# The hybrid decoder step with streamed tiles kept in two halves, even and odd tokens, and matmuls that read one of each in turn

## The chip, the cores and the metric

The kernel runs on one core of one Trainium2 chip. The metric is the device time of one execution in microseconds. Engines are named as the profile names them: PE is TensorE (PEld its weight loads), DVE VectorE, ACT ScalarE, POOL GpSimd, SP the queue that issues most DMAs.

## What is computed

One step of a decoder layer for 256 prompt tokens and 8 x 4 sample tokens, all float32, 2048 wide, feed-forward width 5632:

```
x = x + 1/2 * SwiGLU_1(rmsnorm(x))
h = rmsnorm(x);  z = h @ w_in            # columns: ssm u | q | k | v
y_ssm  = S5 scan of u, gelu, GLU
y_attn = sliding-window attention (window 128), 16 q heads, 4 kv heads
x = x + w_out @ concat(rmsnorm(y_ssm), rmsnorm(y_attn))
x = x + 1/2 * SwiGLU_2(rmsnorm(x))
```

The outputs are the new x, the key and value caches and the states of the scan.

## The kernel before

The activations lie transposed: 128 features on the partitions, the N = 288 tokens along each partition. x is 16 such tiles (KT = 16). All weights come from memory in 680 pieces of 128 x 1024 elements or less, in the order of use; class `Weights` loads each piece (SP queue), and splits it into a rounded high part wh (ScalarE, L89) and a rest wl (VectorE, L90), both of the type fp32r.

Each activation that is multiplied with weights is split likewise. `split_x` does it for x with the norm's gain (xh by ScalarE, L181; xl by VectorE, L182), `up` inside `ffn` for the hidden units (h by VectorE, L308; hh by ScalarE, L309; hl by VectorE, L310), `y_split` inside `mix` for the two mixers' outputs (L678 and L684). A product of a weight and an activation is then three matmuls into one PSUM tile, `mm3` (L273 to L275): wh with the high part, wh with the rest, wl with the high part. The weight block of 128 x 128 is the stationary operand, the activation tile, 288 columns, is the moving one. Every weight block is used for one tile of columns, so each matmul has a weight load beside it.

The stages, in order, are the first SwiGLU (`ffn(0)`, in four chunks of hidden units, each with its part of the down projection), the combined projection with the scan and the attention between its matmuls (`mix`), the output projection, and the second SwiGLU (`ffn(1)`). The order on every engine is that in which the program is written; side work (norms, tables of the scan, softmax) is hung into slots between weight pieces by `Weights.at` and `Weights.spread`. All of `mm3`'s calls stand in `projs`, `down` and the loop over w_out at the end of `mix`. The matmuls of the scan and the attention don't go through `mm3`; they read tiles of their own.

Of the rest of the names: e, p and c5 belong to the tables of the scan (`precompute`), where `er`, `ei` and `c5` hold five powers side by side for each of 32 states, so that `er[:, :, 1]` is 32 elements five apart; `QS` (tile qs) holds the sample tokens' queries with a sequence's elements sixteen apart.

Of the kernel before, what the change touches and what calls it, by code (L numbers as in the profile page):

```python
# [10 lines left out]
F32 = mybir.dt.float32  # L11
F32R = mybir.dt.float32r
I32 = mybir.dt.int32
AF = mybir.ActivationFunctionType
ALU = mybir.AluOpType
# [10 lines left out]
N = T * W1  # L26
# [11 lines left out]
SLOPES = [float(np.float32(2.0 ** (-8.0 * (h + 1) / NH))) for h in range(NH)]  # L38
MAGIC = 1.5 * 2.0 ** 23
TWO_PI = 6.283185005187988  # L40


def heads_of(i):
# [74 lines left out]
def tile_hymba_step(ctx, tc, io):  # L118
    nc = tc.nc
    act, dve, pool_e, pe, sp = nc.scalar, nc.vector, nc.gpsimd, nc.tensor, nc.sync  # L120
# [12 lines left out]
    def ffn_units(l):  # L133
        seq = []
        for c in range(NCK):
            for f in range(CHS[c]):
                if not (c > 0 and f == 0):
                    seq.append(("gu", C0[c] + f))
            if c + 1 < NCK:
                seq.append(("gu", C0[c + 1]))  # L140
            seq.append(("down", c))
        return seq
# [26 lines left out]
    x = [cp.tile([P, N], F32, name="x%d" % k) for k in range(KT)]  # L169
    xh = [cp.tile([P, N], F32R, name="xh%d" % k) for k in range(KT)]  # L170
    cp.tile([P, 32], F32, name="gap_x")
    xl = [cp.tile([P, N], F32R, name="xl%d" % k) for k in range(KT)]
    gains = cp.tile([P, 66], F32, name="gains")
# [4 lines left out]
    cp.tile([P, 56], F32, name="gap_w")  # L178

    def split_x(k, g):  # L180
        act.activation(xh[k], x[k], AF.Copy, scale=gains[:, g:g + 1])  # L181
        dve.scalar_tensor_tensor(xl[k], x[k], gains[:, g:g + 1], xh[k].bitcast(F32),  # L182
                                 op0=ALU.mult, op1=ALU.subtract)

    def square_x(k, first=False, eng=pool_e, acc=acc):
# [72 lines left out]
    for k in range(8):  # L258
        split_x(k, k)
    W.split()  # L260
    W.split()
    for k in range(8, KT):
        split_x(k, k)
# [5 lines left out]
    def mm3(ps, wh, wl, kts, rh, rl, first, last):  # L269
        n = len(kts)  # L270
        for a, k in enumerate(kts):
            s = slice(a * P, (a + 1) * P)
            pe.matmul(ps, wh[:, s], rh[k], start=first and a == 0, stop=False)  # L273
            pe.matmul(ps, wh[:, s], rl[k], start=False, stop=False)  # L274
            pe.matmul(ps, wl[:, s], rh[k], start=False, stop=last and a == n - 1)  # L275

    def projs(n):

        ps = [pm.tile([P, 512], F32, name="main") for _ in range(n)]
        for hf in range(2):  # L280
            for p_ in ps:
                wh, wl = W.next()
                mm3(p_[:, :N], wh, wl, range(8 * hf, 8 * hf + 8), xh, xl, hf == 0, hf == 1)
        return ps

    def proj():
        return projs(1)[0]

    def ffn(l, post, hp, first):
        HH, HL = {}, {}  # L290
        w0 = W.i
        hold = Hold(W.i + first)
        early = [] if l else projs(3)

        def gate(f, pg, s2):
            t1 = tp.tile([P, N], F32, name="t1")
            s1 = tp.tile([P, N], F32, name="s1")
            dve.tensor_tensor(t1, pg[:, :N], R, op=ALU.mult)  # L298
            act.activation(s1, t1, AF.Silu)  # L299
            pool_e.tensor_tensor(s2, s1, R, op=ALU.mult)  # L300

        def up(f, pu, s2):
            h = tp.tile([P, N], F32, name="h")
            hh = hp.tile([P, N], F32R, name="hh")
            if f == 0:
                hp.tile([P, 32], F32, name="gap_r", bufs=1)
            hl = hp.tile([P, N], F32R, name="hl")
            dve.tensor_tensor(h, pu[:, :N], s2, op=ALU.mult)  # L308
            act.copy(hh, h)  # L309
            dve.tensor_tensor(hl, h, hh.bitcast(F32), op=ALU.subtract)  # L310
            HH[f], HL[f] = hh, hl

        def gu(f):
            s2 = tp.tile([P, N], F32, name="s2")
            pg = early.pop(0) if early else proj()
            hold(lambda: gate(f, pg, s2))
            pu = early.pop(0) if early else proj()
            hold(lambda: up(f, pu, s2))

        def down(c):  # L320
            n = CHS[c]
            rh = {k: HH.pop(C0[c] + k) for k in range(n)}
            rl = {k: HL.pop(C0[c] + k) for k in range(n)}
            for d in range(KT):
                ps = pm.tile([P, 512], F32, name="main")
                wh, wl = W.next()
                mm3(ps[:, :N], wh, wl, range(n // 2), rh, rl, True, False)
                wh, wl = W.next()
                mm3(ps[:, :N], wh, wl, range(n // 2, n), rh, rl, False, True)
                dve.scalar_tensor_tensor(x[d], ps[:, :N], 0.5, x[d], op0=ALU.mult, op1=ALU.add)  # L330
                if c == NCK - 1:
                    post(d)

        def gap():

            ps = pm.tile([P, 512], F32, name="main")
            for i in range(2):
                pe.matmul(ps[:, :256], ones, R[:, 8:264], start=i == 0, stop=i == 1)

        W.at(w0 + first + 8, gap)  # L340
        for kind, j in ffn_units(l):
            (gu if kind == "gu" else down)(j)
# [8 lines left out]
    def precompute(qp):  # L351
# [65 lines left out]
        def cos_sin(c, s, f, tmp):  # L417
            act.activation(s, f, AF.Sin, scale=TWO_PI)
            stt(tmp, f, -1.0, f, op0=ALU.mult, op1=ALU.max)
            yield  # L420
            act.activation(c, tmp, AF.Sin, bias=halfpi, scale=-TWO_PI)

# [15 lines left out]
        def common():  # L438
# [34 lines left out]
            yield from cos_sin(c5, ei, f5, g5)  # L473
            act.activation(shalf, f5[:, :, 1], AF.Sin, scale=TWO_PI / 2)
            yield
# [124 lines left out]
    def post_norm(g0):  # L600
        def prep(d):
            split_x(d, g0 + d)
            square_x(d, d == 0)

        def post(d):
            W.at(W.i + (d < KT - 1), prep, d)
        return post
# [10 lines left out]
    with ExitStack() as es:  # L618
        mix(tc, nc, io, es, W, MIX0, dict(
            x=x, xh=xh, xl=xl, gains=gains, ident=ident, ones=ones, acc=acc, R=R, tp=tp,  # L620
# [11 lines left out]
def mix(tc, nc, io, es, W, base, e):  # L632
    act, dve, pool_e, pe = nc.scalar, nc.vector, nc.gpsimd, nc.tensor
    tt, ts, stt = dve.tensor_tensor, dve.tensor_scalar, dve.scalar_tensor_tensor
    x, R, gains, ident, acc = e["x"], e["R"], e["gains"], e["ident"], e["acc"]
# [36 lines left out]
    def y_split(pool, src, g, first, eng=pool_e):  # L672
        hh = pool.tile([P, N], F32R, name="hh", bufs=8)
        if first:
            pool.tile([P, 32], F32, name="gap_y", bufs=1)
        hl = pool.tile([P, N], F32R, name="hl", bufs=8)
        gc = gains[:, g:g + 1]
        act.activation(hh, src, AF.Copy, scale=gc)  # L678
        YH.append(hh)
        YL.append(hl)  # L680
        sq = tp.tile([P, N], F32, name="sq", bufs=3)
        act.activation(sq, src, AF.Square)
        yield
        stt(hl, src, gc, hh.bitcast(F32), op0=ALU.mult, op1=ALU.subtract)  # L684
        if first:
            eng.tensor_copy(acc, sq)
        else:
            eng.tensor_tensor(acc, acc, sq, op=ALU.add)
# [102 lines left out]
    def ssm_glu(j):  # L791
        yn = YN.pop(j)
        ps = aux()
        pe.matmul(ps[:, :N], GL.pop(j), yn, start=True, stop=True)
        t = tp.tile([P, N], F32, name="s1")
        act.activation(t, ps[:, :N], AF.Tanh, scale=0.5)
        yield
        y2 = tp.tile([P, N], F32, name="s2")
        stt(y2, t, 1.0, yn, op0=ALU.add, op1=ALU.mult)
        yield  # L800
        yield from y_split(ys, y2, 48 + j, j == 0, dve if j == 7 else pool_e)
# [14 lines left out]
    for j in range(8):  # L816
        s = base + 2 * j + 5
# [50 lines left out]
    for j in range(8):  # L868
        ps = proj()
# [13 lines left out]
    for p in range(2):  # L883
        ps = proj()
# [120 lines left out]
    def sample(p):  # L1005
# [56 lines left out]
        for g in range(4):  # L1062
            act.copy(tok(YR[4 * p + g], None), src[:, g])
        yield
        todo = [y_split(lp, YR.pop(4 * p + g), 56 + 4 * p + g, p == 0 and g == 0) for g in range(4)]
        for g in range(5):
            for y in todo[max(0, g - 1):g + 1]:
# [3 lines left out]
    for i in range(8):  # L1071
        s = base + 2 * (12 + i) + 2
# [4 lines left out]
    for p in range(2):  # L1077
        s = base + 2 * (12 + 4 * p + 3) + 2
# [4 lines left out]
    for i in range(8):  # L1083
        p, g = divmod(i, 4)
        ps = proj()
# [16 lines left out]
    for hf in range(2):  # L1102
        for d in range(KT):
            if hf and d == 1:
                W.at(W.i, att_norm)
            wh, wl = W.next()
            ps = pm.tile([P, 512], F32, name="main")
# [163 lines left out]
```

## Time and profile before

| | |
|---|---|
| median of 3 runs | 1998.19 us (1997.27 to 2003.86) |
| span of the profiled execution | 1998.1 us |
| instructions | 37634 |
| TensorE busy | 1980.5 us, 99% |
| VectorE, ScalarE, GpSimd busy | 1219.0, 852.0, 296.0 us |
| moved by DMA | 359.04 MB, mean 180 GB/s |

No time besides the span is listed for the profiled execution itself, so the span is what the working below starts from. In a row of a group stand line, engine, operation, output and inputs with their shapes, the count, then busy time in us and the mean of one in ns, then the idle time of the engine before them and what ended it. A row of a stretch has, for each engine, the busy us and the number of instructions, then the granted clock of TensorE, the share of the DMA engines and the GB/s. A row of the timeline has the start and the length in us. Matmuls overlap, so their lengths add up to more than the time they take; the distance of their starts is what one costs.

### The profile page before, as it was taken

The page shows a single profiled execution, that of the slowest core. Times are in us where ns is not written, and L with a number is a line of the kernel's source. Part 1 is how long each engine was busy: PE and PEld are TensorE (multiplying, and loading weights), DVE is VectorE, ACT ScalarE, POOL GpSimd, SP SyncE. Part 2 cuts the span into 40 slices and gives each one's busy share as a digit, 9 for nine tenths or more (in the row PEclk, how much of TensorE's full clock was granted, in tenths as well). Part 3 has the DMA queues.
Part 4 walks back from the last instruction along what each step waited for, and adds up shares of the span by engine and source line. Part 5 has one row for each costly group of instructions (what it writes and reads, how often), then busy time and mean ns, then how long its engine had stood idle before and what let it go on. Part 6 is the DMA issues. An engine that isn't in the chain of part 4 may idle for free.

```text
span 1998.1 us, 37634 instructions
## 1 busy us (share of the span) xinstructions
PE 1980.5 (99%) x15256; PEld 1968.0 (98%) x15256; DVE 1219.0 (61%) x1874; ACT 852.0 (43%) x1334; POOL 296.0 (15%) x450
## 2 busy tenths in 40 slices
PE   8999999999999999999999999999999999999999
PEld 7999999999999999999989999999999999999999
DVE  5577666566666654677888874555555455555554
ACT  5443444443444443543476553333333333333333
POOL 3110011000100000211368640000000000000000
PEclk9999999999999999999999999999999999999999
DMA  7555655546555664678744445555555555555555
GB/s 237 188 169 152 198 168 201 193 151 209 198 180 155 215 201 142 216 248 265 247 132 132 154 159 169 169 155 172 181 169 162 160 186 169 157 157 193 169 154 158
DMA packets 122622, 359.04 MB, mean 180 GB/s; under 512 B 22448, under 2 KB 30256, under 8 KB 121264
## 3 DMA queue, kind: packets, MB, share of 16 engines
q1 hardware_dynamic: 114672, 340.81, 53.5%
q10 hardware_dynamic: 7776, 15.83, 2.3%
q8 instruction: 119, 1.95, 0.4%
q14 instruction: 55, 0.45, 0.1%
HBM read 338.40 MB, written 20.22 MB: 179 GB/s over the span
## 4 chain that ended last, share of the span: by engine, by line
PE 96%; DMA 1%; POOL 1%; DVE 0%; SPq 0%; ACT 0%; issue 0%; POOLq 0%; ACTq 0%; DVEq 0%
PE main L273 31%; PE main L275 31%; PE main L274 31%; POOL acc L191 1%; PE main L733 1%; DMA yd<-yg 0%; PE main L566 0%; PE main L572 0%; DMA x<-in_x 0%; PE main L988 0%; DMA raw<-in_w_gu 0%; PE main L775 0%; PE main L774 0%; PE main L956 0%; PE main L773 0%; PE main L975 0%
## 5 line engine op out<-in xcount | busy, mean ns | idle before, releaser
L90 DVE TENSOR_TENSOR wl<-raw,wh 128x1024 fp32r<-128x1024 f32 (+2 forms) x680 | 758.6, 1116 | 526.2 <-ACT wh L89 521.1
L273 PE MATMUL main<-xh,wh 128*128 128x288 f32 x3136 | 924.4, 295 | 6.7 <-ACT xh L181 6.4
L275 PE MATMUL main<-xh,wl 128*128 128x288 f32 x3136 | 919.0, 293 | 2.2 <-DVE wl L90 2.2
L274 PE MATMUL main<-xl,wh 128*128 128x288 f32 x3136 | 918.4, 293 | 0.6 <-DVE xl L182 0.6
L89 ACT CAST wh<-raw 128x1024 fp32r<-128x1024 f32 (+2 forms) x680 | 643.1, 947 | 600.2 <-PE main L274 385.4
L273 PEld LDWEIGHTS main<-xh,wh 128*128 128x128 f32 x3136 | 589.5, 188 | 8.0 <-ACT xh L181 6.4
L275 PEld LDWEIGHTS main<-xh,wl 128*128 128x128 f32 x3136 | 589.3, 188 | 3.0 <-DVE wl L90 2.9
L274 PEld LDWEIGHTS main<-xl,wh 128*128 128x128 f32 x3136 | 589.5, 188 | 1.4 <-DVE xl L182 1.0
L273 PE MATMUL main<-hh,wh 128*128 128x288 f32 x1664 | 489.8, 294 | 0.0
L274 PE MATMUL main<-hl,wh 128*128 128x288 f32 x1664 | 487.9, 293 | 0.3 <-DVE hl L684 0.3
L275 PE MATMUL main<-hh,wl 128*128 128x288 f32 x1664 | 487.8, 293 | 0.0
L274 PEld LDWEIGHTS main<-hl,wh 128*128 128x128 f32 x1664 | 312.6, 188 | 0.7 <-DVE hl L684 0.5
L273 PEld LDWEIGHTS main<-hh,wh 128*128 128x128 f32 x1664 | 312.5, 188 | 0.5 <-DVE t L1095 0.2
L275 PEld LDWEIGHTS main<-hh,wl 128*128 128x128 f32 x1664 | 312.5, 188 | 0.0
L300 POOL TENSOR_TENSOR s<-s,R 128x288 f32<-128x288 f32 x88 | 71.3, 810 | 1228.0 <-ACT s L299 1228.0
L299 ACT ACTIVATE s<-t 128x288 f32<-128x288 f32 x88 | 39.2, 445 | 233.5 <-DVE t L298 233.5
L309 ACT CAST hh<-h 128x288 fp32r<-128x288 f32 x88 | 38.2, 434 | 235.5 <-DVE h L308 235.5
L330 DVE SCALAR_TENSOR_TENSOR x<-main,x 128x288 f32<-128x288 f32 x128 | 58.4, 456 | 52.3 <-PE main L275 51.1
L308 DVE TENSOR_TENSOR h<-main,s 128x288 f32<-128x288 f32 x88 | 40.2, 457 | 70.3 <-PE main L275 69.9
L298 DVE TENSOR_TENSOR t<-main,R 128x288 f32<-128x288 f32 x88 | 40.2, 457 | 59.4 <-PE main L275 59.2
L310 DVE TENSOR_TENSOR hl<-h,hh 128x288 fp32r<-128x288 f32 x88 | 40.3, 458 | 44.0 <-ACT hh L309 44.0
L191 POOL TENSOR_TENSOR acc<-acc,sq 128x288 f32<-128x288 f32 x45 | 48.4, 1075 | 45.8 <-ACT sq L187 44.4
(266 smaller groups left out, 891.0 us busy)
## 6 DMA issues: line engine op xcount, KB each, us to landing
raw<-in_w_gu SPq DMA_DIRECT2D x352, 512.0 KB, 3.5
raw<-in_w_dn SPq DMA_DIRECT2D x128, 384.0 KB, 3.0
raw<-in_w_dn SPq DMA_DIRECT2D x128, 320.0 KB, 3.0
raw<-in_w_in SPq DMA_DIRECT2D x40, 512.0 KB, 4.7
raw<-in_w_out SPq DMA_DIRECT2D x32, 512.0 KB, 3.4
mats<-stage ACTq DMA_DIRECT2D x8, 1536.0 KB, 7.1
mb<-mats SPq DMA_DIRECT2D x8, 768.0 KB, 5.3
ma<-mats SPq DMA_DIRECT2D x8, 512.0 KB, 4.2
```

The lines of the kernel that those rows point to most:

```text
L89: self.nc.scalar.copy(wh[:, :n], t[:, :n])
L90: self.nc.vector.tensor_tensor(wl[:, :n], t[:, :n], wh[:, :n].bitcast(F32), op=ALU.subtract)
L191: eng.tensor_tensor(acc, acc, sq, op=ALU.add)
L273: pe.matmul(ps, wh[:, s], rh[k], start=first and a == 0, stop=False)
L274: pe.matmul(ps, wh[:, s], rl[k], start=False, stop=False)
L275: pe.matmul(ps, wl[:, s], rh[k], start=False, stop=last and a == n - 1)
L298: dve.tensor_tensor(t1, pg[:, :N], R, op=ALU.mult)
L299: act.activation(s1, t1, AF.Silu)
L300: pool_e.tensor_tensor(s2, s1, R, op=ALU.mult)
L308: dve.tensor_tensor(h, pu[:, :N], s2, op=ALU.mult)
L310: dve.tensor_tensor(hl, h, hh.bitcast(F32), op=ALU.subtract)
L330: dve.scalar_tensor_tensor(x[d], ps[:, :N], 0.5, x[d], op0=ALU.mult, op1=ALU.add)
```

## The change

A tile that the matmuls stream (xh, xl, hh, hl, and the h from which the last two are made) no longer holds its 288 tokens in order. Its first 144 elements are the tokens with even numbers, its last 144 those with odd numbers. The instructions that write these tiles read their sources at every second element (`evens`) and write two runs (`halved`). In `mm3` the moving operand is read through `woven`: element 0 of the first half, element 0 of the second, element 1 of the first, and so on, so that the columns enter the array, and the sums leave it, in the order of tokens as before. x, R, the norms and everything that reads PSUM are as they were. The number of instructions, their order on every engine, the tiles and the DMAs are the same. Line numbers after the change are higher by 15 from L43 on.

```diff
+def evens(ap):
+    return ap.rearrange("p (b a) -> p a b", a=2)
+
+def halved(ap):
+    return ap.rearrange("p (a b) -> p a b", a=2)
+
+def woven(ap):
+    return ap.rearrange("p (a b) -> p b a", a=2)
...
     def split_x(k, g):
-        act.activation(xh[k], x[k], AF.Copy, scale=gains[:, g:g + 1])
-        dve.scalar_tensor_tensor(xl[k], x[k], gains[:, g:g + 1], xh[k].bitcast(F32),
+        act.activation(halved(xh[k]), evens(x[k]), AF.Copy, scale=gains[:, g:g + 1])
+        dve.scalar_tensor_tensor(halved(xl[k]), evens(x[k]), gains[:, g:g + 1], halved(xh[k].bitcast(F32)),
                                  op0=ALU.mult, op1=ALU.subtract)
...
-            pe.matmul(ps, wh[:, s], rh[k], start=first and a == 0, stop=False)
-            pe.matmul(ps, wh[:, s], rl[k], start=False, stop=False)
-            pe.matmul(ps, wl[:, s], rh[k], start=False, stop=last and a == n - 1)
+            pe.matmul(ps, wh[:, s], woven(rh[k]), start=first and a == 0, stop=False)
+            pe.matmul(ps, wh[:, s], woven(rl[k]), start=False, stop=False)
+            pe.matmul(ps, wl[:, s], woven(rh[k]), start=False, stop=last and a == n - 1)
...
-            dve.tensor_tensor(h, pu[:, :N], s2, op=ALU.mult)
+            dve.tensor_tensor(halved(h), evens(pu[:, :N]), evens(s2), op=ALU.mult)
...
-        act.activation(hh, src, AF.Copy, scale=gc)
+        act.activation(halved(hh), evens(src), AF.Copy, scale=gc)
...
-        stt(hl, src, gc, hh.bitcast(F32), op0=ALU.mult, op1=ALU.subtract)
+        stt(halved(hl), evens(src), gc, halved(hh.bitcast(F32)), op0=ALU.mult, op1=ALU.subtract)
```

## The prediction

> **What bounds the kernel now.** I read the page's busy line, clock line and chain first, then the groups by line, then one stretch, then single instructions in it.
>
> ```profile
> span 1998.1 us, 37634 instructions
> ...
> PE 1980.5 (99%) x15256; PEld 1968.0 (98%) x15256; DVE 1219.0 (61%) x1874; ACT 852.0 (43%) x1334; POOL 296.0 (15%) x450
> ...
> PEclk9999999999999999999999999999999999999999
> ...
> PE 96%; DMA 1%; POOL 1%; DVE 0%; SPq 0%; ACT 0%; issue 0%; POOLq 0%; ACTq 0%; DVEq 0%
> ```
>
> TensorE is busy from end to end, its granted clock is full in every slice, and 96% of the chain that ended last is TensorE itself. Its idle time in the whole run is 1998.1 - 1980.5 = 17.6 us. The next engine, VectorE, is at 61%. The sum below is made against this span, 1998.1 us; the median of the three runs, 1998.19 us, is the same to 0.01%.
>
> ```profile
> L273 PE MATMUL main<-xh,wh 128*128 128x288 f32 x3136 | 924.4, 295 | 6.7 <-ACT xh L181 6.4
> L275 PE MATMUL main<-xh,wl 128*128 128x288 f32 x3136 | 919.0, 293 | 2.2 <-DVE wl L90 2.2
> L274 PE MATMUL main<-xl,wh 128*128 128x288 f32 x3136 | 918.4, 293 | 0.6 <-DVE xl L182 0.6
> L273 PE MATMUL main<-hh,wh 128*128 128x288 f32 x1664 | 489.8, 294 | 0.0
> L274 PE MATMUL main<-hl,wh 128*128 128x288 f32 x1664 | 487.9, 293 | 0.3 <-DVE hl L684 0.3
> L275 PE MATMUL main<-hh,wl 128*128 128x288 f32 x1664 | 487.8, 293 | 0.0
> ```
>
> These six groups are all the calls of `mm3`: 3 x 3136 + 3 x 1664 = 14,400 matmuls of 288 columns. Every one of them reads its moving operand in the new order after the change. The mean of 293 ns is the length of one instruction, and they overlap, so what one costs the kernel is read from their starts. A stretch of the second SwiGLU, and three neighbours in it:
>
> ```profile
> 1300.00:1500.00 200.00, 200.00 (x1541) 200.00 (x1540) 101.05 (x119) 75.48 (x92) 8.10 (x10) 1.00 0.55 169
> ...
> 1500.05 0.29 PE L273 MATMUL main<-xh,wh 128*128 128x288 f32 x1
> 1500.18 0.29 PE L274 MATMUL main<-xl,wh 128*128 128x288 f32 x1
> 1500.31 0.29 PE L275 MATMUL main<-xh,wl 128*128 128x288 f32 x1
> ```
>
> 1541 matmuls in 200 us are 129.8 ns from start to start, with no idle time on TensorE and the DMA engines at 55%. So 14,400 x 0.1298 = 1869 us of the span is `mm3`, and 129 us is everything else (the small matmuls of the scan and the attention, and the 17.6 us of idle time). A change in the cost of one streamed column is a change of 14,400 x 288 columns: 0.01 ns on each is 41 us.
>
> How much of the 129.8 ns belongs to the columns? The first matmuls of the run go at another pace:
>
> ```profile
> 8.05 0.44 PE L275 MATMUL main<-xh,wl 128*128 128x288 f32 x1
> ...
> 12.13 0.44 PE L274 MATMUL main<-xl,wh 128*128 128x288 f32 x1
> ```
>
> They are 17 steps apart, 4.08 / 17 = 240 ns each, for the same 288 columns: 0.833 ns a column, just what two array steps would be if the steady pace were 120 ns of columns and 10 ns of something fixed. I take that reading: 0.417 ns a column (120 ns) and about 10 ns besides.
>
> **The change, part by part.** It removes no instruction, adds none and moves none; every engine's list reads as before. What it alters is where elements lie and in which order they are read.
>
> (1) The matmuls' reads. Before, one column follows the other in the tile. Now two columns in succession come from places 144 elements apart, one of each half. No matmul of the run before reads so: all its moving operands are runs of 16 elements and more, but for the two-column ones of L946, which are too short to price. So the price has to be bounded.
>
> From below: if TensorE takes elements from anywhere at the same pace, the cost is 0. Below nothing too: the fixed 10 ns might come from neighbours being read too closely behind each other; taking them all away gives 14,400 x 0.0098 = 141 us less.
>
> From above, the nearest rows are on VectorE. These instructions all handle 32 elements; each pair does the same work, but one member has its 32 elements five apart in the tile (`er[:, :, 1]`, `c5[:, :, 1]`, tile p) or sixteen apart (tile qs), the other has them side by side:
>
> ```profile
> L396 DVE TENSOR_TENSOR p<-tmps,tmpi 128x32 f32<-128x32 f32 x1 | 0.2, 216 | 0.0
> L396 DVE TENSOR_TENSOR s<-tmps,tmpi 128x32 f32<-128x32 f32 x1 | 0.2, 191 | 0.0
> L480 DVE TENSOR_TENSOR tmps<-s,p 128x32 f32<-128x32 f32 x1 | 0.2, 213 | 0.0
> L449 DVE TENSOR_TENSOR s<-prm,s 128x32 f32<-128x32 f32 x1 | 0.2, 189 | 0.0
> L1090 DVE TENSOR_TENSOR qs<-main,R 128x32 f32<-128x32 f32 x8 | 1.6, 202 | 0.0
> L886 DVE TENSOR_TENSOR vT<-main,R 128x32 f32<-128x32 f32 x2 | 0.3, 175 | 0.0
> L310 DVE TENSOR_TENSOR hl<-h,hh 128x288 fp32r<-128x288 f32 x88 | 40.3, 458 | 44.0 <-ACT hh L309 44.0
> ```
>
> Scattered elements cost 25 ns (writing), 24 ns (reading) and 27 ns (writing) more for 32, so about 0.78 ns an element. Side by side an element costs (458 - 191) / (288 - 32) = 1.04 ns. Scattered, the same engine is slower by a factor of 1.75: 1.8 ns an element. This can be carried over to TensorE in three ways:
> - by the ratio: 0.417 x 1.75 = 0.73 ns a column, 210 + 10 = 220 ns a matmul;
> - by the addition: 0.417 + 0.78 = 1.2 ns, 345 + 10 = 355 ns;
> - by the time of one access: 1.8 ns, 518 + 10 = 528 ns.
>
> That last one, 14,400 x (0.528 - 0.1298) = 5734 us more, is the upper end.
>
> I take one element per two array steps: 0.833 ns a column, 240 + 10 = 250 ns. [...] With the fixed part hidden it is 240 ns, with all of the 129.8 ns doubled 260 ns.
>
> [...]
>
> Sum for (1): 14,400 x (250 - 129.8) ns = 1731 us, all on the path, since TensorE waits for nothing in between.
>
> (2) The edits on VectorE and ScalarE that put the halves in place (L181, L182, L308, L678, L684): their inputs are now read at every second element, their outputs written in one run.
>
> ```profile
> L182 DVE SCALAR_TENSOR_TENSOR xl<-x,gains,xh 128x288 fp32r<-128x288 f32 x48 | 32.8, 710 | 0.0
> L308 DVE TENSOR_TENSOR h<-main,s 128x288 f32<-128x288 f32 x88 | 40.2, 457 | 70.3 <-PE main L275 69.9
> L684 DVE SCALAR_TENSOR_TENSOR hl<-s,gains,hh 128x288 fp32r<-128x288 f32 x14 | 10.4, 744 | 0.0
> L181 ACT ACTIVATE xh<-x,gains 128x288 fp32r<-128x288 f32 x48 | 24.1, 529 | 3.9 <-POOL x L1096 3.1 <-DVE x L330 0.6
> ```
>
> At best they cost nothing; at worst 288 x 0.78 = 225 ns each, by the same VectorE rows: 48 + 88 + 16 = 152 instructions, 34 us on VectorE, and 64 instructions (L181, L678), 14 us on ScalarE. In the stretch above VectorE is free for 99 of 200 us and ScalarE for 125, and TensorE's matmuls would leave them twice that. I cost them at nothing. Without that cover, at the start and at the turns between stages, it is a few instructions of 0.2 us, 2 us in all.
>
> (3) The 129 us besides: the small matmuls read as before. Of the 17.6 us of idle time some goes if the stream is slower, since weights then come early: 0 to 17.6 us less. I count 0.
>
> Sum: 1998.1 + 1731 = 3729 us.
>
> **The rivals.**
>
> *No price (not slower).* [...] Then a matmul stays at 129.8 ns, the time at 1998 us within the 0.3% (6 us) that this kernel's measurement can tell from no change; and if the fixed 10 ns goes as well, 1857 us. It decides as soon as the starts stay below 130 ns. [...]
>
> *Part of a price.* Reads run ahead in the 10 ns, or pairs are served together, and a matmul ends between 131 and 235 ns; with the ratio's 220 ns the time is 1998 + 14,400 x 0.0902 = 3297 us. [...]
>
> *A dearer access.* The time of one access counts and not the engine's step. At 355 ns it is 5241 us, at 528 ns 7732 us. For it speaks that 25 ns in 32 elements was seen on three different instructions, whether reading or writing, so it may belong to the memory; against it that the stream now takes a column in 0.417 ns. It also comes to pass if TensorE, idle at every second step, falls back to the pace of its first microseconds (240 instead of 129.8 ns for the same matmul): every step then doubles, 500 ns, 7329 us. [...]
>
> **How the numbers follow.** Half pace, 240 to 260 ns (3585 to 3873 us): 0.46. Part of a price, 2004 to 3585 us: 0.15. A dearer access, above 3873 us: 0.24. No price: 0.12 within 0.3%, and 0.03 faster. The likeliest gives 3729 us, its own range being 3585 to 3873. For the whole I leave out the no-price cases (0.15), the smallest part-prices below 2300 us (0.02) and what lies above 7200 us (0.03): 2300 to 7200 us. Slower is 0.46 + 0.15 + 0.24 = 0.85, the same 0.12, faster 0.03.
>
> **What would show it.** In the trace after, the starts of neighbouring matmuls in the second SwiGLU decide between all cases: 240 to 260 ns for my forecast, 129.8 for the rival without a price, 355 or about 500 for the dearer ones. A stretch of 200 us should hold some 800 matmuls, TensorE should stay busy from end to end, VectorE's and ScalarE's shares should about halve. L308's and L182's counterparts may grow by up to 225 ns without a wait of TensorE on them. If the small matmuls or the waits of TensorE on VectorE took up the difference, step (2) or (3) would be wrong; if the granted clock fell, part of a rival.

## The result and the profile after

The changed kernel takes 1890.03 us (median of 4 runs, 1888.15 to 1892.07). Its ratio to the kernel before is 0.9454, 95% interval 0.9439 to 0.9469: 5.5% faster, where 3729 us were forecast. Before has one run of 2424.86 us among its four; the ratio leaves it out.

The page after, its span, busy line and chain:

```profile
span 1888.7 us, 37634 instructions
...
PE 1864.6 (99%) x15256; PEld 1850.5 (98%) x15256; DVE 1208.9 (64%) x1874; ACT 850.2 (45%) x1334; POOL 301.1 (16%) x450
...
PE 92%; DVE 2%; POOL 2%; DMA 1%; ACT 1%; issue 1%; SPq 0%; POOLq 0%; ACTq 0%; DVEq 0%
```

The same number of instructions, TensorE still busy from end to end, and 109.4 us less. A stretch of the first SwiGLU, the stretch of the second that was shown of before, and three neighbours behind it:

```profile
200.00:400.00 200.00, 200.00 (x1628) 199.69 (x1628) 133.86 (x220) 91.65 (x144) 23.99 (x36) 1.00 0.61 199
1300.00:1500.00 200.00, 200.00 (x1635) 200.00 (x1634) 107.09 (x124) 80.15 (x99) 9.60 (x12) 1.00 0.59 180
...
1500.42 0.29 PE L288 MATMUL main<-hh,wh 128*128 128x288 f32 x1
1500.55 0.29 PE L289 MATMUL main<-hl,wh 128*128 128x288 f32 x1
1500.67 0.29 PE L290 MATMUL main<-hh,wl 128*128 128x288 f32 x1
```

1635 matmuls stand where 1541 stood: 122.3 ns from start to start instead of 129.8. (A stretch also counts a matmul that is under way at its start, so such quotients read up to some 0.6 ns low; averaged start by start, this stretch has 122.5 and 130.0 ns.) 14,400 x 7.5 ns = 108 us is nearly all of the difference. The rest of the run, 1888.7 - 14,400 x 0.1223 = 128 us, is about what it was (129 us). Two smaller things nearly cancel in this sum: the first SwiGLU gained more than 7.5 ns a matmul (1628 in the stretch from 200 to 400 us, where 1523 stood before), and TensorE's idle time grew from 17.6 to 24.1 us (1888.7 - 1864.6). At 0.417 ns a column, which the runs of other widths show below ((162.4 - 122.4) / 96 ns), the columns take 120 ns: 7.5 of the 10 ns that stood beside them are gone, and 2.5 are left.

### The profile page after: what moved, and what is told of

Same layout as the page of the kernel before. It is cut to its first block, busy times and chain, and to the rows that moved or that the text cites. A ratio compares the mean times of both kernels' runs of the same rounds, so it can differ in the third digit from the quotient of the medians.

```text
span 1888.7 us, 37634 instructions
## 1 busy us (share of the span) xinstructions
PE 1864.6 (99%) x15256; PEld 1850.5 (98%) x15256; DVE 1208.9 (64%) x1874; ACT 850.2 (45%) x1334; POOL 301.1 (16%) x450
## 4 chain that ended last, share of the span: by engine, by line
PE 92%; DVE 2%; POOL 2%; DMA 1%; ACT 1%; issue 1%; SPq 0%; POOLq 0%; ACTq 0%; DVEq 0%
PE main L288 30%; PE main L290 30%; PE main L289 29%; DVE wl L105 1%; ACT wh L104 1%; PE main L748 1%; DMA U<-ud 0%; DMA ud<-t 0%; POOL acc L206 0%; PE main L581 0%; PE main L587 0%; POOL x L1111 0%; DMA raw<-in_w_gu 0%; PE main L789 0%; PE main L790 0%
## 5 line engine op out<-in xcount | busy, mean ns | idle before, releaser
L288 PE MATMUL main<-xh,wh 128*128 128x288 f32 x3136 | 904.4, 288 | 7.0 <-ACT xh L196 6.4
L290 PE MATMUL main<-xh,wl 128*128 128x288 f32 x3136 | 898.6, 287 | 3.0 <-DVE wl L105 3.0
L289 PE MATMUL main<-xl,wh 128*128 128x288 f32 x3136 | 898.4, 286 | 0.6 <-DVE xl L197 0.6
L288 PE MATMUL main<-hh,wh 128*128 128x288 f32 x1664 | 478.0, 287 | 1.3 <-DVE t L1110 0.7
L289 PE MATMUL main<-hl,wh 128*128 128x288 f32 x1664 | 476.0, 286 | 0.6 <-DVE hl L699 0.6
L290 PE MATMUL main<-hh,wl 128*128 128x288 f32 x1664 | 476.0, 286 | 0.0
L323 DVE TENSOR_TENSOR h<-main,s 128x288 f32<-128x288 f32 x88 | 40.1, 455 | 55.5 <-PE main L290 55.1
```

What stands on the lines that cost most here:

```text
L288: pe.matmul(ps, wh[:, s], woven(rh[k]), start=first and a == 0, stop=False)
L289: pe.matmul(ps, wh[:, s], woven(rl[k]), start=False, stop=False)
L290: pe.matmul(ps, wl[:, s], woven(rh[k]), start=False, stop=last and a == n - 1)
L323: dve.tensor_tensor(halved(h), evens(pu[:, :N]), evens(s2), op=ALU.mult)
```

## Experiments

**Which half of the change.** Two kernels take it apart, and a third reads in turn without storing halves.

The first leaves tiles in order and only reads them through `woven`:

```diff
-            pe.matmul(ps, wh[:, s], rh[k], start=first and a == 0, stop=False)
+            pe.matmul(ps, wh[:, s], woven(rh[k]), start=first and a == 0, stop=False)
...
```

> Only the order of the matmuls' reads is changed; the tiles keep their tokens in order, so the sums come out for other tokens than they should. If the order of reading is the cause (theory A: a plain read loses time at places it crosses as it runs on, which reading from two far places in turn hides; theory B: a matmul's start is shortened by that order): 122.3 ns from start to start and about 1889 us. If the placing by VectorE and ScalarE is the cause (theory C): 129.8 ns and 1998 us.

The second stores halves as the changed kernel does and reads them in one run (in `mm3`, `woven(rh[k])` becomes `rh[k]` again).

> The tiles are stored in halves, but the matmuls read them as one run, so the sums come out for other tokens than they should. Theories A and B: 129.8 ns and 1998 us. Theory C: 122.3 ns and 1889 us.

Measured: 1889.26 us (ratio 0.9446, 0.9432 to 0.9461) and 1998.36 us (ratio 0.9989, 0.998 to 0.9999). The same stretch in both, reads first, then writes:

```profile
1300.00:1500.00 200.00, 200.00 (x1635) 200.00 (x1635) 106.97 (x125) 80.61 (x99) 9.61 (x12) 1.00 0.57 179
```

```profile
1300.00:1500.00 200.00, 200.00 (x1541) 200.00 (x1540) 100.72 (x118) 75.49 (x92) 8.10 (x10) 1.00 0.54 169
```

The order of reading is the whole effect; storing halves costs and gives nothing that the measurement can tell. Theory C is out.

The third kernel reads pairs in turn and lets the sums fall into PSUM in the same order, so that nothing has to be stored differently:

```diff
-            pe.matmul(ps, wh[:, s], rh[k], start=first and a == 0, stop=False)
+            pe.matmul(turns(ps), wh[:, s], turns(rh[k]), start=first and a == 0, stop=False)
...
+def turns(ap):
+    return ap.rearrange("p (a b c) -> p b a c", a=2, c=2)
```

> Tiles stay in order and VectorE and ScalarE are as before; the matmuls read two elements of each half in turn and write the sums to PSUM in the same order, so that each lands in its own column. If pairs hide what single elements hide and PSUM takes the pairs without delay: 122.3 ns, 1888 us, as fast as the changed kernel. If only single elements in turn help, or if the sums' scattered writing costs as much: 129.8 ns, 1998 us. If scattered writing halves the pace: 240 ns, 3580 us.

Measured: 2769.62 us, ratio 1.3848 (1.3828 to 1.3869). None of the three expectations. Its stretch:

```profile
1900.00:2300.00 400.00, 400.00 (x2165) 400.00 (x2164) 141.93 (x165) 106.81 (x130) 12.07 (x15) 1.00 0.38 121
```

400 us / 2165 = 184.8 ns a matmul. The map of turns below has pairs read in turn with PSUM in order, and 184.7 ns too: it is the reading of pairs that costs, and PSUM takes sums scattered by pairs without a delay that shows beside it. Whether it takes single sums scattered as well, which would have spared the stored halves, no run tried.

**Which orders are cheap.** In the next four kernels only the second SwiGLU is altered, and each ran once; what is read from them are distances within one trace, at a granted clock of 1.00. Every 38 weight pieces `mm3` takes another order, each on a line of its own, for instance

```diff
+                elif seg == 1:  # step 2
+                    pe.matmul(ps[:, :N], w, r.rearrange("p (b a) -> p a b", a=2), start=st, stop=sp_)
```

> Only in the second SwiGLU, each eighth of its weight pieces has another order of reading (its sums are those of other tokens): plain; every 2nd, 4th, 8th, 16th, 48th element and then the next sweep; one of each half in turn; one of each quarter in turn. Distance of starts expected. Plain 129.8 ns, halves 122.3. Theory A with one lost step of 0.417 ns for every 16 elements crossed (18 in 288 make 7.5 ns): step 2: 122.3 + 36 x 0.417 = 137; step 4: 152; step 8: 182; steps 16 and 48: 242; quarters 122.3. Theory B (lost at the start alone): 129.8 or 122.3 for all steps. The price forecast for reads that never use a neighbour: 250 ns from step 4 on.

The rows are answers for one line each: count, shortest, median and longest of one matmul, then first and last start. One operand's matmul is every third, so the distance of starts is (last - first) / 3 / (count - 1). In order: every 2nd, 4th, 8th, 16th, 48th element, halves in turn, quarters in turn. (The first order, plain, is the stretch of 80 us ahead of them.)

```profile
1205.00:1285.00 80.00, 80.00 (x618) 80.00 (x617) 40.80 (x46) 30.73 (x39) 4.86 (x6) 1.00 0.50 169
...
L281 PE MATMUL main<-hh,wh x144: 438/438/438, 1374.1 to 1484.3; 128*128 128x288 f32 x144
L283 PE MATMUL main<-hh,wh x48: 440/442/443, 1485.0 to 1521.9; 128*128 128x288 f32 x48
L285 PE MATMUL main<-xh,wh x144: 421/422/423, 1711.1 to 1816.2; 128*128 128x288 f32 x144
L287 PE MATMUL main<-hh,wh x72: 423/425/427, 1905.2 to 1957.7; 128*128 128x288 f32 x72
L289 PE MATMUL main<-hh,wh x120: 334/335/336, 2168.4 to 2227.9; 128*128 128x288 f32 x120
L291 PE MATMUL main<-hh,wh x40: 286/286/294, 2228.4 to 2242.7; 128*128 128x288 f32 x40
L293 PE MATMUL main<-hh,wh x160: 316/316/318, 2353.4 to 2426.5; 128*128 128x288 f32 x160
```

Plain 129.4 ns; step 2: 257; step 4: 262; step 8: 245; step 16: 246; step 48: 167; halves 122; quarters 153. Scattered reads do cost what the forecast said, 245 to 262 ns against 250. Halves in turn, though not one column lies beside the one before, are no scattered read. Theory A's steps (137, 152, 182, and 122.3 for quarters) and theory B's (one value for all) both fail. The elements crossed don't set the price, since step 2 (257 ns) costs no less than step 16 (246 ns).

> Only in the second SwiGLU, each eighth of its weight pieces is read in another way (wider matmuls repeat the first tokens into columns that nothing uses; with other weights the sums are wrong). Distance of starts. Plain, 288, 384 and 512 columns: if the 7.5 ns are lost along the way, 18 steps for 288 columns, one for each 16 (theory A): 129.8, 172.3, 228.9 ns; if they are lost once at the start (theory B): 129.8, 169.8, 223.1. Halves in turn, 288, 384, 512 columns: 122.3, 162.3, 215.6 by both. [...]

Plain with 384 and 512 columns, halves with 288, 384 and 512, weights at every 8th element (gate and up projections), at every 5th (down projection) and at every 2nd:

```profile
L281 PE MATMUL main<-hh,wh x144: 336/337/338, 1347.6 to 1422.7; 128*128 128x384 f32 x144
L283 PE MATMUL main<-hh,wh x48: 390/391/393, 1423.2 to 1455.7; 128*128 128x512 f32 x48
L285 PE MATMUL main<-hh,wh x120: 286/286/286, 1674.9 to 1718.6; 128*128 128x288 f32 x120
L287 PE MATMUL main<-hh,wh x72: 326/326/326, 1719.0 to 1753.6; 128*128 128x384 f32 x72
L289 PE MATMUL main<-hh,wh x120: 379/379/379, 1928.0 to 2005.1; 128*128 128x512 f32 x120
L291 PE MATMUL main<-xh,wh x240: 401/404/415, 2032.9 to 2206.6; 128*128 128x288 f32 x120
L291 PE MATMUL main<-hh,wh x40: 307/388/398, 2005.7 to 2032.2; 128*128 128x288 f32 x40
L293 PE MATMUL main<-hh,wh x160: 292/295/298, 2226.5 to 2289.9; 128*128 128x288 f32 x160
```

Plain: 175 and 230 ns; halves: 122.4, 162.4 and 216.0, so 0.417 ns for each column from 288 to 384 and 0.419 from there to 512. The difference is 7.5 ns at 288 columns, 12.6 at 384 and 14 at 512: it grows with the columns, and theory B, which had 223 at 512, is out. It doesn't grow in step with them (the wider matmuls read 192 or 256 elements twice), and theory A's 172.3 and 228.9 are missed by 3 and 1 ns. There is one weight load per matmul at each width, and the difference grows all the same; whether the load has a part in it stays open, since a stream without weight loads was not run. Weights with a step come out unevenly beside the 129.8 ns of plain ones: 133 ns where four blocks of five are read at every 2nd, 227 at every 5th and 242 at every 8th.

> Only in the second SwiGLU, each eighth of its weight pieces has another order of moving reads (sums of other tokens): runs of 2, 4, 8 and 16 elements from each half in turn; then single elements in turn from two neighbouring blocks of 4, 8, 16 and 48 elements. The step map gave 257, 262, 245, 246 ns for steps 2, 4, 8, 16, 167 for step 48, 153 for quarters, 122.3 for halves. Reuse theory (a pair of neighbours is fetched for two columns' time; a few fetched pairs are kept while other places are read, so with two places in turn each pair is still fetched once, with 18 places it is lost before its second use): all eight orders 122 to 130 ns. Bank theory (two columns in succession collide when their places share a bank, near ones do, those 144 apart don't): runs 122 to 130; neighbouring blocks of 4, 8, 16 like the steps 4, 8, 16: 262, 245, 246; of 48 like step 48: 167.

Runs of 2, 4, 8, 16 from each half, then neighbouring blocks of 4, 8, 16, 48 in turn:

```profile
1205.00:1335.00 130.00, 130.00 (x704) 129.90 (x703) 45.80 (x52) 36.20 (x45) 5.62 (x7) 1.00 0.35 117
...
L281 PE MATMUL main<-hh,wh x144: 302/302/303, 1384.0 to 1442.7; 128*128 128x288 f32 x144
L283 PE MATMUL main<-hh,wh x48: 299/302/303, 1443.1 to 1462.3; 128*128 128x288 f32 x48
L285 PE MATMUL main<-hh,wh x120: 302/302/302, 1620.2 to 1669.0; 128*128 128x288 f32 x120
L287 PE MATMUL main<-hh,wh x72: 286/286/287, 1669.4 to 1695.5; 128*128 128x288 f32 x72
L289 PE MATMUL main<-hh,wh x120: 286/286/286, 1813.5 to 1857.2; 128*128 128x288 f32 x120
L291 PE MATMUL main<-hh,wh x40: 286/286/286, 1857.6 to 1871.9; 128*128 128x288 f32 x40
L293 PE MATMUL main<-hh,wh x160: 286/286/286, 1978.1 to 2036.5; 128*128 128x288 f32 x160
```

Runs: 184.7, 137, 136 and 137 ns. Blocks: 122.4 for all four. Distance is of no account: turns between elements 4 apart are as good as 144 apart, so the bank theory falls. The reuse theory (122 to 130 ns for all eight) holds for the blocks, but is at least 55 ns off for runs of 2 and 6 for the longer runs.

**What a cheap order has in common.** Write the columns as pairs, 0.83 ns each at 0.417 ns a column. Halves: (0,144) (1,145) (2,146) (3,147), four pairs on the same two groups of four neighbours, then two new groups. Plain: (0,1) (2,3), two pairs on a group, then the next. Step 2 and more: every pair on a new group. Theory L counts just that, theory P only that there are two places in turn. Pairs and groups of four are a way of counting that sorts the measured orders; no run shows them in the engine. Groups of two don't sort: halves (122.4 ns) and blocks of 2 (129.4 ns, below) would both have two pairs on a group. Nor do groups of eight: plain (129.8 ns) and blocks of 4 (122.4 ns) would both have four.

> Only in the second SwiGLU, each eighth of its weight pieces has another order of moving reads (sums of other tokens). Two theories fit most orders so far. Theory P: two places in turn hide a loss that one running place shows. Theory L: columns are taken two at a time; a pair that needs a line of four neighbours other than the pair ahead waits one double step (0.83 ns) unless a pair that stays on its lines stands behind it, and even then a little; so each line should serve four pairs in a row (halves) rather than two (plain), and one pair for each line costs 0.83 ns. Expected, P and L: neighbouring blocks of 2 (0,2,1,3,4,6,5,7): 122.4 and 130; blocks of 6: 122.4 and 126 to 130; each element twice, from one place: 126 (half the crossings) and 122.4; each four times: 124 and 122.4; eighths in turn: 153 as quarters, and 153 if all eight lines are kept or 242 if they are not; step 3: 257 and 245 to 262. 512 columns starting at element 1, so that every second pair lies on two lines: 230 and clearly more, up to 350; starting at element 2: 230 and 230.

In order: blocks of 2, blocks of 6, each element twice, each four times, eighths in turn, step 3, 512 columns starting at element 1 and at element 2:

```profile
1205.00:1285.00 80.00, 80.00 (x618) 80.00 (x616) 40.28 (x46) 31.70 (x39) 4.86 (x6) 1.00 0.54 166
...
L281 PE MATMUL main<-xh,wh x112: 285/285/285, 1286.4 to 1327.2; 128*128 128x288 f32 x112
L283 PE MATMUL main<-xh,wh x240: 286/286/286, 1398.1 to 1486.0; 128*128 128x288 f32 x120
L285 PE MATMUL main<-xh,wh x144: 286/286/286, 1486.3 to 1538.9; 128*128 128x288 f32 x144
L287 PE MATMUL main<-xh,wh x208: 427/427/428, 1637.3 to 1792.6; 128*128 128x288 f32 x104
L289 PE MATMUL main<-xh,wh x112: 433/435/436, 1793.3 to 1878.8; 128*128 128x288 f32 x112
L291 PE MATMUL main<-xh,wh x240: 401/402/404, 2000.8 to 2172.9; 128*128 128x512 f32 x120
L293 PE MATMUL main<-xh,wh x48: 395/396/401, 2173.6 to 2206.5; 128*128 128x512 f32 x48
```

Blocks of 2 take 80 us / 618 = 129.4 ns, to the digit what plain takes: two places in turn with only two pairs on a group bring nothing. Theory P, which had 122.4, is out. Each element twice, from one single place, is as fast as halves (122.5), as L had it. Blocks of 6 are fast as well (122.5; L had 126 to 130): a group there serves four pairs, though not in one go. Eighths (250) and step 3 (257) are the full price; columns starting at elements 1 and 2 cost 10 and 3 ns more than the 230 at 0, where L expected clearly more at 1 and nothing at 2.

L comes closest, then, and its sizes are only in part right. On this stream the pace goes with the number of pairs that fall on a group of four neighbours before the read leaves it: four or more, 122.4 ns; two, 129 to 137; one, 245 to 262. Turns between more groups cost more: beside the 122.4 ns of halves, quarters, four groups at a time, take 31 ns more, step 48, six groups at a time, 44, and eighths the full 128. What in the engine makes it so no run shows, nor why plain takes 7.5 ns more than halves, runs of 4 to 16 take 14 more, and runs of 2, whose groups have two pairs with others between, 62.

**One matmul of three.** Only the product with wl reads halves in turn:

```diff
-            pe.matmul(ps, wl[:, s], rh[k], start=False, stop=last and a == n - 1)
+            pe.matmul(ps, wl[:, s], woven(rh[k]), start=False, stop=last and a == n - 1)
```

> Before, with only the third matmul of mm3 (weights' rest with the high part) reading halves in turn; its sums are those of other tokens. If the gain belongs to each matmul by itself: 4800 x 7.5 ns = 36 us less, 1962 us. If it comes from the stream as a whole (a pace that the engine keeps as a state): 1998 or 1889 us.

Measured: 1974.07 us beside 1999.16 of before, ratio 0.9875 (0.9858 to 0.9891): 25 us, neither 36 nor nothing. The stretch of the second SwiGLU, one of the first, and that of the first in the kernel before:

```profile
1300.00:1500.00 200.00, 200.00 (x1553) 200.00 (x1553) 101.63 (x121) 76.78 (x94) 8.10 (x10) 1.00 0.56 173
...
200.00:400.00 200.00, 200.00 (x1549) 199.69 (x1548) 127.37 (x208) 88.20 (x140) 20.02 (x30) 1.00 0.59 190
...
200.00:400.00 200.00, 200.00 (x1523) 199.68 (x1522) 125.94 (x206) 86.72 (x137) 17.02 (x27) 1.00 0.58 190
```

In the second SwiGLU three matmuls take 3 x 200 / 1553 = 386.4 ns instead of 389.4, 3 ns less and not 7.5. That alone would be 4800 x 3 ns = 14 us. In the first they take 387.3 ns instead of 394.0 (with a few small matmuls among them in both), 6.6 ns less. The starts, averaged by line where they lie less than 0.2 us apart, tell where the rest stays. In the second SwiGLU the one that reads in turn is followed after 122.8 ns, the two plain ones after 132.3 and 131.7, where before had 130.0 for each: with one in turn among them the plain ones take some 2 ns more than in a row of their kind. In the first SwiGLU plain ones lose less by it (132.3 and 131.5 ns, before 131.2 and 131.4), and the third gains more (122.9, before 131.2). Why, and why plain reads cost more there to begin with, is open.

## Why the prediction was wrong

- *What bounds the kernel.* Right: all of the change is in the distance of starts of 14,400 matmuls, and 0.01 ns a column is 41 us.
- *Step (1), the price of the reads.* This failed, in its sign. It took the price of elements that lie apart (VectorE's rows, five and sixteen apart) for a read that comes back to each place with the next pair. For reads that don't come back so soon, the 250 ns were right: steps 2 to 16 measured 245 to 262. But no run before the change shows its term, two whole steps for a column by where it is read; it was the author's estimate, and in its place the runs showed, beside those steps, 153 ns for quarters, 167 for step 48, 185 for pairs in turn and 122.3 for halves. Whether the carrying over from VectorE or chance brought it to 250 no run tells. For halves in turn the price is less than nothing, -7.5 ns. The cases without a price came nearest, and were given 0.15. Not all other moving operands are runs of 16 and more, either: L1021's are runs of 8 and L1010's two single columns, in 12 small matmuls.
- *The split of the 129.8 ns.* 120 ns of columns was right, at the 0.417 ns a column that the widths show; "about 10 ns of something fixed" was not. Some 2.5 ns are fixed: halves in turn leave 2.4, 2.4 and 2.7 ns beside the columns at 288, 384 and 512. The other 7.5 grow with the columns (14 at 512). The sentence on "below nothing" pointed the right way, to 1857 us (141 us less); 109 us came. Its supposition, neighbours read too closely behind each other, doesn't fit the maps: each element twice reads them no less closely and takes 122.5 ns, and blocks of 2 in turn gain nothing (129.4). It got 0.03, since nothing in the trace before showed that a plain read can lose anything. The one hint was that the first matmuls, at 240 ns, showed nothing beside their columns where the steady ones showed 10 ns, and it was booked as fixed.
- *Step (2).* Right in that it is hidden, and too high at its worst: VectorE's instructions didn't grow, ScalarE's by 32 ns (529 and 534 before), not by up to 225. Among them L323 reads PSUM at every second element, which "The change" passes over; it costs nothing either:

```profile
L197 DVE SCALAR_TENSOR_TENSOR xl<-x,gains,xh 128x288 fp32r<-128x288 f32 x48 | 32.3, 699 | 0.3 <-ACT xh L196 0.3
L323 DVE TENSOR_TENSOR h<-main,s 128x288 f32<-128x288 f32 x88 | 40.1, 455 | 55.5 <-PE main L290 55.1
L196 ACT ACTIVATE xh<-x,gains 128x288 fp32r<-128x288 f32 x48 | 25.6, 561 | 10.1 <-POOL x L1111 9.4 <-DVE x L345 0.8
L693 ACT ACTIVATE hh<-s,gains 128x288 fp32r<-128x288 f32 x14 | 7.9, 566 | 0.0
```

- *Step (3).* Right in sum: 129 us before, 128 after. Of the idle time in it 0 to 17.6 us less were expected, with a slower stream; the faster one has 6.5 us more.
- *The dearer access.* No. The granted clock stayed full (0.999), and no order of 288 columns cost more than 262 ns.

## What to carry to other kernels

Where TensorE streams fp32r tiles back to back, compare the distance of starts with what the columns alone take: a matmul of 288 columns stood at 129.8 ns with 120 of columns (0.417 ns each), and 7.5 ns of that difference were 5.5% of the kernel. Reading the tile so that two columns in succession come from two places, each walked element by element, took the loss away here (122.4 ns with two halves or with neighbouring blocks of 4 to 48, but 129.4 with blocks of 2), and the instructions that write the tile did the permutation on engines that had time (VectorE busy for 64% of the span, ScalarE for 45%). A step in the moving operand, even of 2, doubled the matmul (245 to 262 ns at steps 2 to 16), so here a permutation belonged into the writing and not into a read with a step.

## What was not expected of the hardware

- A plain, contiguous read was not the fastest: 129.8 ns against 122.4 for 288 columns, 230 against 216 for 512 (256 elements read twice).
- Two elements of each half in turn cost 185 ns, one of each 122.4.
- Turns between blocks of 4 to 144 elements are equally fast (122.4 to 122.5 ns), and blocks of 2 equal to plain (129.4).
- Weights read with a step made the matmuls longer than 129.8 ns: 133 ns at step 2 (four blocks of five), 227 at step 5, 242 at step 8.
